# A fp32 encoder trunk on one core: warming PE without ACT, summing a weight by transfers in the last product, and another order for the last rows and for the step behind the attention

## The chip, the cores and the metric

The kernel runs on one core of one Trainium2 chip. The metric is the device time of one execution in microseconds; a lower one is better. Three runs of the kernel before took 1899.04, 1899.11 and 1897.82 us, with a median of 1899.04. The engines are called as the profile calls them: PE multiplies matrices, DVE works elementwise, ACT evaluates functions and scaled copies, POOL and SP are used here only to issue transfers (POOL those that add to what lies in the target).

## The reference

The input is one sequence of 512 tokens of 1024 float32 features. Two layers run one after the other:

```python
x += 1/2 * SwiGLU(RMSNorm(x))                       # 1024 -> 2 x 2816 -> 1024
x += W_o(g_na * NA(h) W_na + g_f * FNet(h) W_f)     # h = RMSNorm(x)
x += 1/2 * SwiGLU(RMSNorm(x))
```

NA is attention of 8 heads over a neighbourhood in a grid of 8 x 64 tokens, with a learned bias; FNet is the real part of a 2-D Fourier transform; `g_na` and `g_f` are sigmoid gates. At the end stands one more RMSNorm with a gain: out = x * rsqrt(mean(x^2) + 1e-6) * gain. Everything is float32.

## The kernel before

**Products.** A float32 product is made of three matmuls: each operand is split into a rounded part (`hi`) and the rest (`lo`), and PE adds hi x hi, hi x lo and lo x hi (L470, L471, L473 in `product`, L294 to L296 in `mm3`). The large products use Strassen's scheme: seven products in place of eight, each of sums of blocks, with results in the groups of PSUM banks that the profile calls A, B, C (in the mixer) and o (in the out products).

**Weights.** All weights come in granules of 128 x 1024 floats, in one written order (`stage_items`, the nested `strassen` writes the order of the seven products). `Stream` walks it: `load` issues the transfer from SP (`raw`, L147), `prep` makes `whi` on ACT (L178, or L173 for a negated one) and `wlo` on DVE (L181 or L174). Three buffers exist for each of `whi` and `wlo`, and weights are prepared two items ahead of the product that reads them. Some weights are sums of two granules. There are three ways to make them: a load with a second transfer that POOL issues with accumulation (L149); an addition on DVE (`summed`, L163); or, with `then`, an accumulating transfer that POOL issues behind the `wlo` of an earlier item that used the same granule (L183), so that the granule d + a of product 6 becomes d + a + b for product 3. `dma=True` chooses the last way; in `before` the mixer's products use it and the FFN's do not.

**Order of instructions.** A scheduler orders each engine's instructions; inside `tc.manual_schedule` the engines named keep the order of the code, and `tc.issue_after` puts a block behind a given instruction.

**Stages.** Each layer has an FFN, the mixer and another FFN. `stage_ffn` runs the five column groups of the inner layer, then the out products, in the passes (1), (2), (5, 6, 7, 3), (4), each over three chunks c = 0 to 2 of the inner dimension; `update` adds a result to `x` (L701). In the last FFN (`late`) the end is the final norm: `squares` sums x^2 by ACT (L337), `inverse` gives the factor of a block of 128 rows by a square root on ACT and small DVE operations (L389 to L404), `gained` multiplies x by the gain on DVE (L961), `scaled` multiplies that by the factor on ACT and sends it out (L966, L967), and `whole` does both multiplications on DVE (L973, L974). The last product runs block by block (`by_block`), so that row blocks 0 and 1 finish last, one behind the other.

**End of the attention.** In `stage_mixer`, the results of the last two attention heads are split on ACT (L1284) and DVE (L1287) into `o`; two weights of the out projection of the attention (`fill`, two granules n) are prepared; and the operands t1, t2, t3 of the gates' Strassen products are made from blocks of the normed input: a difference `t` on DVE (L1418), its `hi` on ACT (L1641), its `lo` on DVE (L1646). In the rest of the text wlo1 and wlo2 are the two weights of the fill, whi3 and whi4 those of the gates' first product, and so on in the order of the stream. Behind the fill follow the gates' products A, B, C (`gate_block`); ACT takes snapshots of the PSUM results (`sn`, L540).

**Start.** L128 to L135: `ones` and `warm` are set by DVE, ACT loads its function table with a tanh that writes into `warm`, and nine matmuls of `warm` by itself keep PE busy until the first weights and the first parts of the transposed input (`xt`) are there.

Of the kernel before, what the change touches and what calls it, by code (L numbers as in the profile page):

```python
# [17 lines left out]
P = 128  # L18
D = 1024
T = 512  # L20
L = 2
# [5 lines left out]
NH, DH = 8, 64  # L27
EPS = 1e-6
NEG = -1.0e30
WARM = 9  # L30
AHEAD = 2
ORDER = (1, 5, 2, 6, 7, 3, 4)
FETCH = 8
# [56 lines left out]
def encoder_kernel(  # L90
# [15 lines left out]
    def nm(s):  # L106
        uid[0] += 1
        return f"{s}_{uid[0]}"
# [17 lines left out]
    idents = cp.tile([P, 2, P], F32, tag="ident", name="ident")  # L126
    ident, mirror = idents[:, 0, :], idents[:, 1, :]
    ones = cp.tile([P, 1], F32, tag="ones", name="ones")  # L128
    V.memset(ones, 1.0)
    warm = slot(BF16, "warm", (T,))  # L130
    V.memset(warm, 0.0)
    S.activation(warm[:, 0:1], ones, AF.Tanh)
    pw = bank()
    for _ in range(WARM):
        PE.matmul(pw, warm[:, 0:P], warm, start=True, stop=True)  # L135
# [50 lines left out]
    def stage_items():  # L186
        items, st = [], 0

        def add(*a, **k):
            items.append(Item(*a, stage=st, **k))  # L190

        def strassen(s, name, idx, sizes, order, dma=False, behind=None):
            def key(q, g):
                return (s, name(q), idx, g) if g < 2 else (s, "h" + q, idx, 0)

            r = {}
            for q, q2 in (("a", None), ("b", None), ("c", "a"), ("d", "c")):
                r[q] = [Raw(key(q, g), n, q2 and key(q2, g)) for g, n in enumerate(sizes)]
            d2 = [Raw(key("d", g), n) for g, n in enumerate(sizes)]
            for m in order:  # L200
                for g in range(len(sizes)):
                    a, b, c, d = [r[q][g] for q in "abcd"]
                    if m == 1:
                        add(a, neg=True)
                    elif m == 2:
                        add(b)
                    elif m == 3:
                        add(d, None if dma else b)
                    elif m == 4:
                        add(d2[g])  # L210
                    elif m == 5:
                        add(d)
                    elif m == 6:
                        add(d, a, then=b.key if dma else None)
                    else:
                        add(c)
                for key in (behind or {}).get(m, ()):
                    add(Raw(key))

        def out_sizes(c):  # L220
            return (1024, 512) if c == 0 else (1024, 1024)

        def ffn(s):
            first = not items
            if first:
                for g in range(4):
                    add(Raw((s, "cl", g)), parts=2 if g < 2 else 1, pieces=2 if g == 0 else 1)
            for j in range(NB):
                order = (1, 2, 5, 6, 7, 3, 4) if first and j == 0 else (1, 5, 6, 2, 7, 3, 4)
                strassen(s, lambda q: q, j, (1024,) * (2 if first or j else 3), order)  # L230
            for order in ((1,), (2,), (5, 6, 7, 3), (4,)):
                for c in range(3):
                    strassen(s, lambda q: "o" + q, c, out_sizes(c), order)

        for l in range(L):
            ffn((l, 1))
            st += 1
            s = (l, 0)
            two = (1024, 1024)
            qk = [(s, "qk", g) for g in range(8)]  # L240
            strassen(s, lambda q: "u" + q, 0, two, (1, 5, 6, 2, 3, 7, 4), True, behind={5: qk[0:1], 6: qk[1:2], 2: qk[2:3], 3: qk[3:4], 7: qk[4:5]})
            for key in qk[5:] + [(s, "f", g) for g in range(4)]:
                add(Raw(key))
            st += 1
            for g in range(2):
                add(Raw((s, "n", 0, g)))
            st += 1
            for i in range(2):
                strassen(s, lambda q: "g" + q, i, two, ORDER, True)
            for g in range(2):  # L250
                add(Raw((s, "n", 1, g)))
            strassen(s, lambda q: "w" + q, 0, two, ORDER, True)
            ffn((l, 2))
        return items

    class Stream:
# [27 lines left out]
        def next(self, ahead=AHEAD):  # L284
            self.prep(self.pos + 1 + ahead)
            it = self.items[self.pos]
            self.pos += 1
            return it.out
# [288 lines left out]
    def stage_ffn(norm, nxt, late):  # L577
# [120 lines left out]
        def update(ps, i, j, sign, bs=(0, 1)):  # L698
            for b in bs:
                v = x[:, 2 * j + b, i * T : (i + 1) * T]  # L700
                V.scalar_tensor_tensor(v, ps[b], 0.25 * sign, v, ALU.mult, ALU.add)  # L701
# [155 lines left out]
        for i, (m, c, _) in enumerate(steps):  # L857
# [24 lines left out]
            make(i + 2)  # L882
            if i == 6 and not late:
                nxt.quad(0, 0)
            if m == 4 and c == 1:
                update(ps[1], 1, 0, 1)
            if m == 4 and c == 0 and late:
                gf[0] = slot(F32, "gf", (D,))
                nc.sync.dma_start(out=gf[0], in_=bass.AP(tensor=gfin.tensor, offset=gfin.offset, ap=[[0, P], [1, D]]))
            if c < 2:  # L890
                continue
            if m == 1:
                update(ps[1], 0, 0, -1)
            elif m == 2:
                update(ps[2], 0, 0, 1)
                nxt.squares(0, 0)
            elif m == 5:
                update(ps[5], 0, 1, 1)
                update(ps[5], 1, 1, -1)
            elif m == 6:  # L900
                update(ps[1], 1, 1, 1)
            elif m == 7:
                update(ps[7], 1, 1, 1)
                nxt.squares(1, 1)
                update(ps[1], 0, 1, -1)
            elif m == 3:
                update(ps[3], 0, 1, 1)
                nxt.squares(0, 1)
                if late:
                    make(i + 3)  # L910
            elif late:
                with (
                    tc.issue_after(ws.items[-1].last.ins),
                    tc.manual_schedule(engines={mybir.EngineType.DVE, mybir.EngineType.Activation}),
                ):
                    ready = nxt.inverses(2)
                    next(ready)
                    gained(2, 0)
                    next(ready)
                    gained(2, 1)  # L920
                    for _ in ready:
                        pass
                    scaled(nxt, 2)
                    update(ps[7], 1, 0, 1, (0,))
                    nxt.squares(1, 0, (0,))
                    root = [nxt.inverse(b, *nxt.terms(b)) for b in range(2)]
                    next(root[0])
                    gained(3, 0)
                    gained(3, 1)
                    scaled(nxt, 3)  # L930
                    update(ps[7], 1, 0, 1, (1,))
                    nxt.squares(1, 0, (1,))
                    next(root[1])
                    next(root[0])
                    gained(0, 0)
                    next(root[0])
                    gained(0, 1)
                    scaled(nxt, 0)
                    next(root[1])
                    next(root[1])  # L940
                    whole(nxt, 1, 0)
                    whole(nxt, 1, 1)
            else:
                update(ps[7], 1, 0, 1)
                if not nxt.mix:
                    nxt.squares(1, 0)
                nxt.later((1, 0))
# [4 lines left out]
    def half(tb, i=None):  # L952
        c = slice(0, D) if i is None else slice(i * T, (i + 1) * T)
        return ob[tb][:, c], x[:, tb, c], gf[0][:, c], out[:, tb, c]

    def gained(tb, i):

        if tb not in ob:
            ob[tb] = slot(F32, "o", (D,))
        o_, v, g, _ = half(tb, i)  # L960
        V.tensor_tensor(o_, v, g, ALU.mult)  # L961

    def scaled(norm, tb):

        o_, _, _, to = half(tb)
        S.activation(o_, o_, AF.Copy, scale=norm.inv[tb])  # L966
        nc.sync.dma_start(out=to, in_=o_)  # L967

    def whole(norm, tb, i):
        if tb not in ob:  # L970
            ob[tb] = slot(F32, "o", (D,))
        o_, v, g, to = half(tb, i)
        V.scalar_tensor_tensor(o_, v, norm.inv[tb], g, ALU.mult, ALU.mult)  # L973
        nc.sync.dma_start(out=to, in_=o_)  # L974


    def stage_mixer(l, norm, nxt):
# [454 lines left out]
        with tc.manual_schedule(engines={mybir.EngineType.DVE, mybir.EngineType.Activation}):  # L1432
            with tc.manual_schedule(engines={mybir.EngineType.PE}):
# [194 lines left out]
                pt_[7] = [h() for h in ph]  # L1628
                ws.prep(ws.pos + 1)
                f_copy(1, 3, rows_of(yf, 3, second_f), True)  # L1630
                t12, _ = next(first)
                o.append(hilo("o"))
                po = [att_pv(i, pt_.pop(i)) for i in (6, 7)]
                att_split(6, po[0])
                att_split(7, po[1])
        ws.prep(ws.pos + 2)
        acts = {1: (hx[0], lx[0], 0), 2: (hx[1], lx[1], 0), 3: (hx[1], lx[1], 256), 4: (hx[0], lx[0], 256)}

        def high(src, s):
# [285 lines left out]
```

## Time and profile before

| What | us |
|---|---|
| median of three runs | 1899.04 |
| profiled execution, whole time | 1898.17 |
| profiled execution, span | 1896.4 |
| PE busy | 1884.2 (99%) |
| DVE busy | 1647.8 (87%) |
| ACT busy | 1189.4 (63%) |
| POOL busy | 171.5 (9%) |
| mean granted clock of PE | 0.999 |

A line of the time order reads: start in us from the span's start, duration in us, engine, line of the kernel, operation, output <- inputs, shapes, and x with the number of instructions that are taken together. Where the engine stood idle before, a bracket gives for how long and what released it. In the rows of transfers the duration is that of issuing; how long one takes to land stands in a line of its own, as minimum, median and maximum.

### The profile page before, as it was taken

What the parts mean: (1) busy time and instruction counts of PE and PEld (TensorE: products, weight loads), DVE (VectorE), ACT (ScalarE), POOL (GpSimd) and SP (SyncE); (2) the same over time, 40 slices, a digit from 0 to 9 for tenths busy, and PEclk for the clock granted to TensorE, in tenths of its full rate; (3) what the DMA queues carried; (4) which work ended last, traced back from release to release, by engine and by line L of the source; (5) the groups of instructions that cost most, each with busy time, mean ns of one, the idle gap of its engine ahead of it and who ended that gap; (6) DMA issues with size and microseconds to landing.
All of it is one profiled execution on the core that took longest, in us unless ns stands there. A gap on an engine that the chain in (4) does not pass through costs nothing.

```text
span 1896.4 us, 25088 instructions
## 1 busy us (share of the span) xinstructions
PE 1884.2 (99%) x9149; PEld 1579.3 (83%) x9149; DVE 1647.8 (87%) x2006; ACT 1189.4 (63%) x1700; POOL 171.5 (9%) x210
## 2 busy tenths in 40 slices
PE   9999999999999999999999999999999999999998
PEld 7888888888888888888888888888888888888886
DVE  7877899788989977889997778998989899887898
ACT  6655665668666755566665556666685576556664
POOL 0101011100111011001010100101001101100010
PEclk9999999999999999999999999999999999999999
DMA  9777498932886777649877664988248767766594
GB/s 302 202 201 194 148 247 265 225 106 97 248 218 165 183 188 205 175 154 263 250 184 213 185 181 152 268 273 204 84 139 238 206 167 179 207 175 178 173 283 137
DMA packets 106939, 372.74 MB, mean 197 GB/s; under 512 B 12288, under 2 KB 12416, under 8 KB 106816
## 3 DMA queue, kind: packets, MB, share of 16 engines
q1 hardware_dynamic: 78144, 272.80, 41.9%
q0 software_dynamic: 28528, 98.33, 28.4%
q8 instruction: 71, 1.16, 0.2%
q14 instruction: 52, 0.43, 0.1%
q10 hardware_dynamic: 144, 0.02, 0.0%
HBM read 365.85 MB, written 2.11 MB: 194 GB/s over the span
## 4 chain that ended last, share of the span: by engine, by line
PE 98%; DVE 1%; issue 0%; ACT 0%; DVEq 0%; ACTq 0%
PE A L470 10%; PE A L471 10%; PE A L473 10%; PE o L470 7%; PE o L473 7%; PE o L471 7%; PE B L470 5%; PE B L471 5%; PE B L473 5%; PE ps L295 4%; PE ps L294 4%; PE ps L296 3%; PE C L471 2%; PE C L470 2%; PE C L473 2%; PE tr L593 2%
## 5 line engine op out<-in xcount | busy, mean ns | idle before, releaser
L178 ACT ACTIVATE whi<-raw 128x1024 fp32r<-128x1024 f32 (+1 forms) x536 | 553.6, 1037 | 387.1 <-PE A L471 123.4
L181 DVE TENSOR_TENSOR wlo<-raw,whi 128x1024 fp32r<-128x1024 f32 (+1 forms) x536 | 636.2, 1193 | 167.7 <-ACT whi L178 166.1
L149 POOL DMA_DIRECT2D raw<-in_wst_dram x166 | 144.4, 895 | 1375.5 <-DMA raw<-in_wst_dram 846.1
L163 DVE TENSOR_TENSOR raw<-raw,raw 128x1024 f32<-128x1024 f32 (+1 forms) x150 | 177.5, 1191 | 1.2
L471 PE MATMUL A<-whi,xl 128*128 128x512 f32 x400 | 155.7, 389 | 0.0
L470 PE MATMUL A<-whi,xh 128*128 128x512 f32 x400 | 155.7, 389 | 0.0
L473 PE MATMUL A<-wlo,xh 128*128 128x512 f32 x400 | 115.1, 389 | 0.0
L173 ACT ACTIVATE whi<-raw 128x1024 fp32r<-128x1024 f32 (+1 forms) x83 | 85.8, 1036 | 43.0 <-PE o L471 12.8
L174 DVE SCALAR_TENSOR_TENSOR wlo<-raw,whi 128x1024 fp32r<-128x1024 f32 (+1 forms) x83 | 98.0, 1195 | 13.1 <-ACT whi L173 13.1
L675 ACT ACTIVATE th<-sn,rh 128x512 f32<-128x512 f32 x80 | 56.9, 714 | 69.2 <-DVE sn L545 69.2
L540 ACT ACTIVATE sn<-A 128x512 f32<-128x512 f32 x104 | 60.7, 588 | 46.4 <-PE A L473 46.3
L473 PEld LDWEIGHTS A<-wlo,xh 128*128 128x128 f32 x400 | 75.1, 188 | 15.6
L471 PEld LDWEIGHTS A<-whi,xl 128*128 128x128 f32 x400 | 75.1, 188 | 15.4
L470 PEld LDWEIGHTS A<-whi,xh 128*128 128x128 f32 x400 | 75.1, 188 | 15.4
L470 PE MATMUL C<-whi,xh 128*128 128x512 f32 x208 | 81.1, 390 | 0.0
L471 PE MATMUL C<-whi,xl 128*128 128x512 f32 x208 | 81.0, 389 | 0.0
L471 PE MATMUL B<-whi,xl 128*128 128x512 f32 x208 | 81.0, 389 | 0.0
L470 PE MATMUL B<-whi,xh 128*128 128x512 f32 x208 | 80.9, 389 | 0.0
L473 PE MATMUL C<-wlo,xh 128*128 128x512 f32 x208 | 59.8, 389 | 0.0
L473 PE MATMUL B<-wlo,xh 128*128 128x512 f32 x208 | 59.8, 389 | 0.0
L470 PE MATMUL B<-whi,t5h 128*128 128x512 f32 x136 | 54.2, 399 | 0.0
L695 DVE TENSOR_TENSOR at<-at,at 128x1024 f32<-128x1024 f32 (+1 forms) x48 | 53.8, 1130 | 0.0
(446 smaller groups left out, 4783.9 us busy)
## 6 DMA issues: line engine op xcount, KB each, us to landing
raw<-in_wst_dram SPq DMA_DIRECT2D x470, 512.0 KB, 5.3
raw<-in_wst_dram POOLq DMA_DIRECT2D x174, 512.0 KB, 8.0
raw<-in_wst_dram SPq DMA_DIRECT2D x30, 256.0 KB, 3.9
bm<-in_bias_dram SPq DMA_DIRECT2D x16, 384.0 KB, 3.8
vs<-v SPq DMA_DIRECT2D x12, 256.0 KB, 3.8
x<-in_xin_dram SPq DMA_DIRECT2D x4, 512.0 KB, 10.2
raw<-in_wst_dram POOLq DMA_DIRECT2D x8, 256.0 KB, 8.1
dft<-in_dft_dram POOLq DMA_DIRECT2D x8, 256.0 KB, 4.2
```

The costliest lines, as they stand in the source:

```text
L149: G.dma_start(out=self.t, in_=wst[GRAN_AT[self.plus]][:, 0 : self.n], accum_op=ALU.add)
L163: V.tensor_tensor(self.raw.t, self.raw.t, self.add.t, ALU.add)
L173: S.activation(hi, t, AF.Copy, scale=-1.0)
L174: self.last = V.scalar_tensor_tensor(lo, t, -1.0, hi.bitcast(F32), ALU.mult, ALU.subtract)
L178: S.activation(hi[:, cs], t[:, cs], AF.Copy)
L181: self.last = V.tensor_tensor(lo[:, cs], t[:, cs], hi[:, cs].bitcast(F32), ALU.subtract)
L294: PE.matmul(ps, lh, rh, start=start, stop=False, skip_group_check=again)
L295: PE.matmul(ps, lh, rl, start=False, stop=False, skip_group_check=again)
L470: PE.matmul(ps, lh, rh, start=start, stop=False, skip_group_check=again)
L471: PE.matmul(ps, ll, rh, start=False, stop=False, skip_group_check=again)
L473: PE.matmul(ps, lh, rl, start=False, stop=stop, skip_group_check=again)
L540: S.activation(t[:, b, :], ps[b], AF.Copy)
```

## The change

- `WARM` goes from 9 to 10. `warm` is set ahead of `ones`, and the tanh writes into a small tile `sq` instead of `warm`, so the warm matmuls no longer read anything that ACT wrote.
- In the last FFN, the out products' chunk c = 2 uses `dma=True`: product 3's weights d + a + b come by two transfers of POOL (L183) instead of two loads by SP and two additions by DVE (L163).
- At the end of the last FFN, the gain's products for row blocks 2 and 3 (`gained`) move ahead of the last weight; the update of ps[1] moves from chunk 1 of product 4 to the end, one half for each block; row blocks 2 and 3 are scaled by ACT; of row block 0, ACT scales one half and DVE (a new `tensor_scalar`) the other; of row block 1, DVE finishes one half (`whole`) and ACT scales the other and issues its output transfer itself. Outputs go by SP as two transfers of 512 KB and three of 256 KB and by ACT as one of 256 KB; before, they were three of 512 KB and two of 256 KB, all by SP.
- In the mixer, `ws.prep(ws.pos + 2)` moves ahead of the split of the last two heads, and `next(first)`, which issues the subtraction `t`, behind it.

```diff
-WARM = 9
+WARM = 10
...
-    V.memset(ones, 1.0)
     warm = slot(BF16, "warm", (T,))
     V.memset(warm, 0.0)
-    S.activation(warm[:, 0:1], ones, AF.Tanh)
+    V.memset(ones, 1.0)
+    S.activation(sp.tile([P, 8], F32, tag="sq", name=nm("sq"), bufs=2)[:, 0:1], ones, AF.Tanh)
...
-                    strassen(s, lambda q: "o" + q, c, out_sizes(c), order)
+                    strassen(s, lambda q: "o" + q, c, out_sizes(c), order, last and c == 2)
...
-            ffn((l, 2))
+            ffn((l, 2), l == L - 1)
...
-            if m == 4 and c == 1:
+            if m == 4 and c == 1 and not late:
                 update(ps[1], 1, 0, 1)
             if m == 4 and c == 0 and late:
...
+                with (
+                    tc.issue_after(ws.items[ws.prepped - 1].last.ins),
+                    tc.manual_schedule(engines={mybir.EngineType.DVE}),
+                ):
+                    for tb in (2, 3):
+                        gained(tb, 0)
+                        gained(tb, 1)
...
                     next(ready)
-                    gained(2, 0)
                     next(ready)
-                    gained(2, 1)
+                    gained(0, 0)
                     for _ in ready:
                         pass
                     scaled(nxt, 2)
+                    scaled(nxt, 3)
+                    update(ps[1], 1, 0, 1, (0,))
+                    root = [nxt.inverse(b, *nxt.terms(b)) for b in range(2)]
                     update(ps[7], 1, 0, 1, (0,))
                     nxt.squares(1, 0, (0,))
-                    root = [nxt.inverse(b, *nxt.terms(b)) for b in range(2)]
                     next(root[0])
-                    gained(3, 0)
-                    gained(3, 1)
-                    scaled(nxt, 3)
+                    gained(0, 1)
+                    gained(1, 0)
+                    update(ps[1], 1, 0, 1, (1,))
                     update(ps[7], 1, 0, 1, (1,))
                     nxt.squares(1, 0, (1,))
                     next(root[1])
                     next(root[0])
-                    gained(0, 0)
                     next(root[0])
-                    gained(0, 1)
-                    scaled(nxt, 0)
+                    scaled(nxt, 0, 0)
+                    o_, _, _, to = half(0, 1)
+                    V.tensor_scalar(o_, o_, nxt.inv[0], None, ALU.mult)
+                    nc.sync.dma_start(out=to, in_=o_)
                     next(root[1])
                     next(root[1])
-                    whole(nxt, 1, 0)
                     whole(nxt, 1, 1)
+                    scaled(nxt, 1, 0, nc.scalar)
...
-    def scaled(norm, tb):
-
-        o_, _, _, to = half(tb)
+    def scaled(norm, tb, i=None, by=nc.sync):
+
+        o_, _, _, to = half(tb, i)
         S.activation(o_, o_, AF.Copy, scale=norm.inv[tb])
-        nc.sync.dma_start(out=to, in_=o_)
+        by.dma_start(out=to, in_=o_)
...
                 f_copy(1, 3, rows_of(yf, 3, second_f), True)
-                t12, _ = next(first)
                 o.append(hilo("o"))
                 po = [att_pv(i, pt_.pop(i)) for i in (6, 7)]
+                ws.prep(ws.pos + 2)
                 att_split(6, po[0])
                 att_split(7, po[1])
-        ws.prep(ws.pos + 2)
+                t12, _ = next(first)
```

More of the change, by code (lines that the diff above doesn't have):

```diff
@@ L221, in out_sizes, with ffn @@
             return (1024, 512) if c == 0 else (1024, 1024)
-        def ffn(s):
+        def ffn(s, last=False):
             first = not items
```

## The prediction

> **What bounds the kernel now.** I read the shares of the page first, then the waits of PE, then the time order of each engine at the four places that the change touches. The profiled execution took 1898.17 us (span 1896.4 us), 0.87 us below the median of the three runs shown, 1899.04 us; the sum below is made against the execution and set on the median.
>
> ```profile
> PE 1884.2 (99%) x9149; PEld 1579.3 (83%) x9149; DVE 1647.8 (87%) x2006; ACT 1189.4 (63%) x1700; POOL 171.5 (9%) x210
> PE ps L135 <- ACT warm L132: 2.7, 1, 2.7
> ```
>
> PE is busy 99%; its only listed wait is the one at the start, and 8.9 us separate its end (1887.5, where DVE's last wait on it ends, quoted below) from the span's. So a saving on DVE, ACT, SP or POOL is worth nothing unless it shortens the start or what follows PE's last product, while a delay of a weight or a snapshot past the matmul that needs it is added in full: nothing later gives it back. I take the four places in order of time.
>
> **Start: 0 us.** The zeroing of `warm` goes ahead of the one of `ones`, the tanh writes another tile, and a tenth warm matmul is added.
>
> ```profile
> 0.90 0.27 DVE L131 MEMSET warm<- 128x256 uint32 x1
> 2.73 4.02 PE L135 MATMUL ps<-warm 128*128 128x512 bf16 x9 [2.73 <-ACT warm L132]
> 4.81 0.61 ACT L178 ACTIVATE whi<-raw 128x512 fp32r<-128x512 f32 x1
> 6.19 0.99 PE L470 MATMUL cl<-whi,xh 128*128 128x512 f32 x1
> 8.57 0.73 ACT L303 ACTIVATE xh<-xt,gn 128x512 fp32r<-128x512 f32 x1 [2.31 <-DMA xt<-in_xtr_dram]
> 9.33 0.75 DVE L304 SCALAR_TENSOR_TENSOR xl<-xt,gn,xh 128x512 fp32r<-128x512 f32 x1
> 10.14 0.19 PEld L471 LDWEIGHTS cl<-whi,xl 128*128 128x128 f32 x1 [0.35 <-DVE xl L304]
> ```
>
> PE's warming then starts at about 0.81+0.27 = 1.1 instead of 2.73. Ten matmuls at 4.02/9 = 0.45 us end near 5.6, after the first weights are ready (4.81+0.61 = 5.42), so real work starts some 0.6 us before 6.19. It then runs into the wait that already stands at 10.14: the second part of `xt` lands (8.57), ACT makes `xh`, DVE makes `xl` (9.33+0.75 = 10.08). Neither the transfer nor the two operations move, so the 0.6 us becomes idle time ahead of 10.14. The tenth matmul (0.45 us) lies in the same gap. Bounds: all of the 0.6 if the wait went too, +0.3 if the tenth matmul held back what the wait leaves; the row of the wait decides for 0.
>
> **Behind the attention, once in each layer: +1.9 us each, +3.8 us together.** No word of the change's summary names it, but the subtraction `t` (L1418) and the preparation of the fill's second weight change places. On DVE the order wlo1, t, o x4, wlo2, wlo3 becomes wlo1, wlo2, o x4, t, wlo3. ACT's order up to whi6 stays: whi2, o x4, t1h, whi3, (DVE's block) t2h, whi4, fs x4, whi5, whi6. Layer 1:
>
> ```profile
> 478.90 1.72 DVE L1287 TENSOR_TENSOR o<-ps,o 64x256 fp32r<-64x256 f32 x4
> 481.79 1.22 DVE L174 SCALAR_TENSOR_TENSOR wlo<-raw,whi 128x1024 fp32r<-128x1024 f32 x1
> 492.91 2.36 DVE L181 TENSOR_TENSOR wlo<-raw,whi 128x1024 fp32r<-128x1024 f32 x2 [1.62 <-ACT whi L178]
> 502.00 2.52 DVE L181 TENSOR_TENSOR wlo<-raw,whi 128x1024 fp32r<-128x1024 f32 x2
> ```
>
> ```profile
> 476.84 1.07 ACT L178 ACTIVATE whi<-raw 128x1024 fp32r<-128x1024 f32 x1
> 479.37 1.06 ACT L1641 ACTIVATE t1h<-t 128x1024 fp32r<-128x1024 f32 x1
> 487.84 1.06 ACT L1641 ACTIVATE t2h<-t 128x1024 fp32r<-128x1024 f32 x1 [6.46 <-DVE t L1656]
> 488.80 1.05 ACT L173 ACTIVATE whi<-raw 128x1024 fp32r<-128x1024 f32 x1
> 491.80 2.03 ACT L178 ACTIVATE whi<-raw 128x1024 fp32r<-128x1024 f32 x2
> 510.60 1.06 ACT L178 ACTIVATE whi<-raw 128x1024 fp32r<-128x1024 f32 x1 [0.31 <-PE A L471]
> 511.56 0.58 ACT L540 ACTIVATE sn<-A 128x512 f32<-128x512 f32 x1
> ```
>
> Step by step: whi2 ends at 477.91, so wlo2 runs from 477.95 and `o` follows at 479.1 for 1.72; `t` starts at 480.84 and ends at 482.06 (before: its result was there when ACT reached t1h at 479.37). t1h goes to 482.1 (+2.7), whi3 behind it to 483.1, and wlo3, which needs whi3, to 484.16 against 481.79: +2.37. The three windows below (us, then busy us of PE, weight loads, DVE, ACT, POOL) show DVE without a hole in what follows:
>
> ```profile
> 476.60:491.20 14.60, 14.49 (x68) 11.68 (x67) 14.46 (x16) 8.05 (x13) 1.71 (x2) 1.00 1.05 307
> 493.00:504.50 11.50, 11.50 (x52) 9.52 (x51) 11.43 (x10) 8.04 (x10) 0.85 (x1) 1.00 0.49 147
> 1857.00:1882.60 25.60, 25.60 (x115) 21.20 (x114) 25.60 (x30) 13.23 (x19) 0.00 (x0) 1.00 0.29 98
> ```
>
> So t2h (487.84) and whi4 behind it (488.80) also come 2.37 later, whi4 ending at 492.2; whi5 goes from 491.80 to 494.1, ends at 495.2, and wlo5 starts there, 2.3 after 492.91. From there DVE had no hole up to wlo9 (502.00): +2.25. Behind its wlo9 hangs POOL's transfer:
>
> ```profile
> 503.51 0.85 POOL L183 DMA_DIRECT2D raw<-in_wst_dram  x1 [16.38 <-DVE wlo L181]
> 1444.00 0.85 POOL L183 DMA_DIRECT2D raw<-in_wst_dram  x1 [19.59 <-DVE wlo L181]
> DMA to landing us min/median/max: 6.8/7.7/8.6
> DMA to landing us min/median/max: 5.5/7.7/12.6
> ```
>
> ```profile
> 491.81 0.39 PE L470 MATMUL A<-whi,xh 128*128 128x512 f32 x1
> 494.53 0.39 PE L470 MATMUL B<-whi,t1h 128*128 128x512 f32 x1
> 512.21 0.49 PE L470 MATMUL A<-whi,t3h 128*128 128x512 f32 x1
> ```
>
> The first landing line is for the two L183 transfers of this place, the second for all sixteen. What PE sees: in the fill it can gain up to the 0.1 us that it lacks in the first window, since wlo2 comes early; at 491.81 it waits for whi4 until 492.2, +0.4; at 494.53 it waits for whi5 until 495.2, +0.7 in all. At 512.21 PE had no slack: it waits for the second snapshot (511.56), which on ACT stands behind the weight (510.60) that waits for POOL's transfer. Issued at 505.75 and landing 6.8 us later, at 512.5, it gives whi until 513.5, the snapshot until 514.1, PE at 514.1: +1.9. That contains the 0.7. Layer 2 runs the same code 940.5 us later (its POOL transfer at 1444.00), so +3.8 us for both.
>
> Bounds: the landing has the widest spread. With 5.5 us PE goes on at 512.9, and what stands is the +0.7 of B: +0.7 per layer. With the median of all, 7.7, it is +2.9, with 8.6 it is +3.8. I take 6.8, the row of this very transfer. Below nothing lies only the fill's 0.1. The Trainium skill, "DMA: Bandwidth & Descriptors", section "Anatomy of one DMA — SWDGE (gpsimd) path", gives such a transfer 2.0 us and its bytes over 436 GB/s, an estimate of 3.2 us for 512 KB; by it the transfer would be off the path and the two layers would cost 1.4 us, but the rows have 5.5 at the least.
>
> **Last out product, c = 2: 0 us.** The two additions L163 leave DVE, SP loses two loads of 512 KB, POOL gains two accumulating transfers behind product 6's weights.
>
> ```profile
> 1853.50 1.22 DVE L181 TENSOR_TENSOR wlo<-raw,whi 128x1024 fp32r<-128x1024 f32 x1
> 1860.17 1.22 DVE L163 TENSOR_TENSOR raw<-raw,raw 128x1024 f32<-128x1024 f32 x1
> 1878.04 3.49 DVE L181 TENSOR_TENSOR wlo<-raw,whi 128x1024 fp32r<-128x1024 f32 x3
> ```
>
> ```profile
> 1884.16 0.62 PE L473 MATMUL o<-wlo,c4h 128*128 128x512 f32 x2
> ```
>
> DVE has no hole in the third window above and saves 2 x 1.14 us; four products with the gains of rows 2 and 3 (4 x 0.6 us), which stood behind the last weight, now stand ahead of it. So that weight ends near 1882, as before, about 2 us ahead of the last pair of matmuls at 1884.16 that reads it. The first transfer starts behind product 6's wlo (1853.50 + 1.22), about 1855, the second some 2 us later; with 5.5 to 8.6 us the first lands between 1860.5 and 1863.6, where the sum that it replaces ended at 1861.4. PE has no wait there now; what is late first is the last weight, with 2 us of cover. SP's and POOL's queues have nothing else due in that stretch that PE waits for.
>
> **Behind the last product: -1.0 us.** Here every DVE operation counts.
>
> ```profile
> 1887.54 0.69 DVE L701 SCALAR_TENSOR_TENSOR x<-o,x 128x512 f32<-128x512 f32 x1 [0.33 <-PE o L473]
> 1888.33 0.67 DVE L961 TENSOR_TENSOR o<-x,gf 128x512 f32<-128x512 f32 x1
> ...
> 1890.83 1.42 DVE L973 SCALAR_TENSOR_TENSOR o<-x,inv,gf 128x512 f32<-128x512 f32 x2
> 1891.67 1.21 SPq L974 DMA_DIRECT2D out_dram<-o  x2
> ```
>
> Two products with the gain (0.6 each, the one at 1888.33 and a second like it) leave the stretch behind 1887.54, one of the two L973 halves (0.6) goes to ACT, and one 128x512 product by `inv` (0.6) comes in: -1.2. The moved update of ps[1] (0.6) stands just ahead of the last one and may delay it by 0.1. DVE's last half then ends near 1891.1 and its output is issued there, against 1892.27 (the second of the two issues at 1891.67): -1.1. ACT's two halves of 0.6 us should end by 1891, and the one that ACT issues itself lands with the other. I take -1.0. Bounds: -1.2 if ACT stays clear, +0.5 if ACT's two halves and its own issue end last.
>
> **Sum.** 0 + 3.8 + 0 - 1.0 = +2.8 us: the profiled execution would take 1901.0 and, set on the median, 1901.8 us (+0.15%). About 0.2% (3.8 us: 1895.2 to 1902.8) is what a measurement of this kernel can tell from no change, so the likeliest answer is "same", near its upper end.
>
> **The rivals.** Slower: the accumulating transfer lands late. Its place is POOL's issue near 505.75 and its twin near 1446; each us of landing is a us per layer. It decides from a landing of 7.2 us (2.3 per layer): barely above the 6.8 forecast, and below the 7.7 median. At 7.7 the sum is 2 x 2.9 - 1.0 = +4.8, 1903.8 us; at 8.6, 1905.6. For it: the median, and that SP's loads, held back by the same weights, then run beside it; against it: both transfers of the nearest place took under 7. Chance 0.33.
>
> Cheap: the transfer lands early, or the second snapshot doesn't stand behind it, and only B's +0.7 is left: 1.4 - 1.0 = +0.4, 1899.4 us. For it the 5.5 row; chance 0.13.
>
> Faster: the wait for t1h is no wait, the layers gain the fill's 0.1 each, and the tail gives its -1.2: -1.4, 1897.6 us, still within 0.2%. The start would have to give its whole 1.6 us of earlier warming, and more, to pass the bound. Against it stand the 10.14 wait and DVE's closed row. Chance 0.08, a third of it past the bound.
>
> Late last weight: product 3's transfers take over 9 us, ACT's weights come 1 to 2 us late and the last weight uses up its cover; +1 us on the forecast, 1902.8. Chance 0.04.
>
> **How the numbers follow.** The forecast has 0.42. Within 0.2%: 0.42 + 0.13 + 0.05 + 0.02 = 0.62; slower: 0.33 + 0.02 = 0.35; faster: 0.03. The range runs from the faster rival, 1897.6, to the 8.6 us landing, 1905.6. The likeliest one's own range is 1900.8 to 1902.8.
>
> **What will show it.** In the changed profile: warm matmuls from 1.1 and the `xl` wait still near 10.1; t1h at 482.1 with an idle time of over 2 us before it, released by DVE `t`; wlo3 at 484.2; a PE wait of over 1 us near 512, released by ACT's snapshot, in both layers; PE's end near 1891.3; no L163 at 1860 to 1864; the last SP issue 3.6 us after PE's end instead of 4.8. Wrong it would be if ACT made t1h without that wait, if the transfer landed clearly off 6.8 us, or if PE waited between 1860 and 1887.

## The result and the profile after

The changed kernel took 1903.72 us (median of 10 runs, 1902.30 to 1905.44) against 1899.23 us (10 runs) for the kernel before: a ratio of 1.0023 with a 95% interval of 1.0015 to 1.0032, so +4.5 us. The forecast was 1901.8 with a range of 1897.6 to 1905.6: the time lies in the range and on the side that was forecast, but past the 1902.8 (0.2%) at which the likeliest case ended. The profiled execution took 1902.30 us, 4.13 us more than the one of before.

Behind the attention, layer 1. The first fence has the waits of PE in the changed kernel (in all us, times, longest), the others the time order of DVE, ACT, POOL and PE there.

```profile
PE A L470 <- ACT sn L540: 1.4, 2, 0.8
PE A L470 <- ACT whi L173: 1.4, 2, 0.7
PE o L473 <- DVE wlo L181: 0.3, 1, 0.3
```

```profile
479.87 1.23 DVE L1427 TENSOR_TENSOR t<-t,t 128x1024 f32<-128x1024 f32 x1
483.17 1.23 DVE L174 SCALAR_TENSOR_TENSOR wlo<-raw,whi 128x1024 fp32r<-128x1024 f32 x1 [2.08 <-ACT whi L173]
```

```profile
481.13 1.06 ACT L1650 ACTIVATE t1h<-t 128x1024 fp32r<-128x1024 f32 x1 [2.76 <-DVE t L1427]
490.19 1.04 ACT L173 ACTIVATE whi<-raw 128x1024 fp32r<-128x1024 f32 x1
511.34 1.06 ACT L178 ACTIVATE whi<-raw 128x1024 fp32r<-128x1024 f32 x1 [1.13 <-DMA raw<-in_wst_dram]
512.30 0.58 ACT L540 ACTIVATE sn<-A 128x512 f32<-128x512 f32 x1
```

```profile
504.90 0.85 POOL L183 DMA_DIRECT2D raw<-in_wst_dram  x1 [18.72 <-DVE wlo L181]
```

```profile
491.28 0.50 PE L470 MATMUL A<-whi,xh 128*128 128x512 f32 x1 [0.67 <-ACT whi L173]
494.31 0.50 PE L470 MATMUL B<-whi,t1h 128*128 128x512 f32 x1
512.93 0.50 PE L470 MATMUL A<-whi,t3h 128*128 128x512 f32 x1 [0.65 <-ACT sn L540]
```

This execution is 0.99 us ahead at the fill, because of its start (below). With that added, t1h starts at 482.12 (forecast 482.1), wlo3 at 484.16 (484.16), POOL's transfer is issued at 505.89 (505.75), and PE goes on at 513.92 (514.1). The chain came out as it was laid out: ACT waits 2.76 us for DVE's `t`, DVE 2.08 us for whi3, ACT 1.13 us for the landing, PE for the snapshot. The landing took 6.33 us where 6.8 was forecast, and PE followed it by 1.70 where 1.6 was.

The last out product and the end. First the window up to PE's end in the kernel before and the one in the changed kernel (us, then busy us of PE, weight loads, DVE, ACT and POOL), then rows of the changed kernel from the time order of the four engines and SP's queue, the rows between left out.

```profile
1857.00:1887.50 30.50, 30.50 (x135) 24.93 (x133) 29.95 (x45) 15.76 (x25) 0.00 (x0) 1.00 0.27 92
1861.00:1891.20 30.20, 29.89 (x130) 23.88 (x129) 28.50 (x45) 15.34 (x22) 0.86 (x1) 1.00 0.32 88
```

```profile
1868.15 1.23 DVE L181 TENSOR_TENSOR wlo<-raw,whi 128x1024 fp32r<-128x1024 f32 x1 [1.12 <-ACT whi L178]
1869.82 2.01 ACT L178 ACTIVATE whi<-raw 128x1024 fp32r<-128x1024 f32 x2 [1.70 <-DMA raw<-in_wst_dram]
1884.13 2.48 DVE L970 TENSOR_TENSOR o<-x,gf 128x512 f32<-128x512 f32 x4
1886.54 1.21 DVE L181 TENSOR_TENSOR wlo<-raw,whi 128x1024 fp32r<-128x1024 f32 x1
1887.80 0.73 PE L473 MATMUL o<-wlo,c4h 128*128 128x512 f32 x2 [0.31 <-DVE wlo L181]
1890.65 0.61 PE L473 MATMUL o<-wlo,c4h 128*128 128x512 f32 x2
1892.22 1.48 DVE L701 SCALAR_TENSOR_TENSOR x<-o,x 128x512 f32<-128x512 f32 x2
1896.54 0.33 SPq L983 DMA_DIRECT2D out_dram<-o  x1
```

DVE, which was idle for 0.55 us of this stretch before (30.50 - 29.95), now stands idle for 1.70 us of it (30.20 - 28.50), above all for weights that ACT makes from POOL's two transfers; the four products with the gain come next, the last weight is made at 1886.54, PE waits for it, and when PE ends (1891.28) DVE's last two updates have not begun: the first starts at 1892.22. The last output issue stands 5.26 us behind PE's end; before it was 4.76.

The next table sets the starts of the same matmuls in two traces against each other: by how many us PE falls behind (or, with a minus, gets ahead of) the first look at the kernel before, place by place. A look is one profiled execution; "exchange alone" and "exchange undone" are the first and the fifth experiment.

| Place | after | after, 2nd look | exchange alone | exchange undone | before, 2nd look |
|---|---|---|---|---|---|
| start (up to 30 us) | -0.94 | -0.54 | -0.69 | -1.00 | -0.56 |
| 30 us to the fill, layer 1 | -0.05 | +0.07 | +0.23 | +0.39 | +0.09 |
| fill, layers 1 and 2 | -0.37, -0.38 | -0.39, -0.36 | -0.34, -0.38 | 0, 0 | 0, 0 |
| whi4 and whi5, layers 1 and 2 | +1.27, +1.33 | +1.30, +1.27 | +1.25, +1.30 | 0, 0 | 0, 0 |
| second t3h block, layers 1 and 2 | +0.82, +0.97 | +1.27, +0.72 | +1.37, +1.48 | 0, +0.91 | 0, +0.68 |
| between the layers' places | +0.33 | -0.15 | -0.12 | -0.05 | +0.09 |
| 1453 to 1875 us | -0.04 | +0.05 | -0.05 | +0.09 | +0.13 |
| last product, c = 2 | +0.83 | +0.78 | +1.25 | +0.06 | +0.14 |
| behind PE | +0.36 | +0.33 | -0.05 | +0.33 | -0.01 |
| end of the span | +4.13 | +4.35 | +5.25 | +0.73 | +0.54 |

### The profile page after: what moved, and what is told of

Same layout as the page of the kernel before. It is cut to its first block, busy times and chain, and to the rows that moved or that the text cites. A ratio compares the mean times of both kernels' runs of the same rounds, so it can differ in the third digit from the quotient of the medians.

```text
span 1900.5 us, 25094 instructions
## 1 busy us (share of the span) xinstructions
PE 1886.2 (99%) x9150; PEld 1578.8 (83%) x9150; DVE 1645.6 (87%) x2005; ACT 1188.6 (63%) x1701; POOL 173.4 (9%) x212
## 4 chain that ended last, share of the span: by engine, by line
PE 93%; issue 2%; DMA 2%; DVE 1%; ACT 0%; POOL 0%; SPq 0%; POOLq 0%; DVEq 0%; ACTq 0%
PE A L470 10%; PE A L471 10%; PE A L473 9%; PE o L470 7%; PE o L471 7%; PE o L473 7%; PE B L470 5%; PE B L471 5%; PE B L473 5%; PE ps L294 3%; PE ps L295 3%; PE ps L296 3%; PE C L471 2%; PE C L470 2%; PE C L473 2%
## 5 line engine op out<-in xcount | busy, mean ns | idle before, releaser
L163 DVE TENSOR_TENSOR raw<-raw,raw 128x1024 f32<-128x1024 f32 (+1 forms) x148 | 174.8, 1189 | 1.2
```

The lines of the kernel that those rows point to most:

```text
L163: V.tensor_tensor(self.raw.t, self.raw.t, self.add.t, ALU.add)
```

## The experiments

The ratios are the recorded ones, with their 95% intervals; they are not the quotients of the two medians beside them and differ from these by up to 0.0005.

**The exchange alone.**

```diff
                 f_copy(1, 3, rows_of(yf, 3, second_f), True)
-                t12, _ = next(first)
                 o.append(hilo("o"))
                 po = [att_pv(i, pt_.pop(i)) for i in (6, 7)]
+                ws.prep(ws.pos + 2)
                 att_split(6, po[0])
                 att_split(7, po[1])
-        ws.prep(ws.pos + 2)
+                t12, _ = next(first)
```

> The kernel before with the exchange behind the attention alone. Theory M (the prediction's step: t1h waits for t, and the second snapshot of product A waits behind the weight that POOL's transfer brings): +3.4 to +3.8 us, PE 1.7 to 1.9 us later at the second t3h block of each layer, nothing elsewhere. Rival (the delay comes from other places that the changed kernel shifted too, and the exchange itself is covered): under +1.5 us.

Measured: 1903.43 us against 1898.63, ratio 1.0028 (1.0017 to 1.0039): as much as the whole change. The table has 2.28 and 2.40 us for the two layers, more than the 1.7 to 1.9 expected. It also has +1.25 us in the last product, which no theory had; there PE waited for another operand:

```profile
PE o L471 <- DVE c4l L301: 0.9, 1, 0.9
```

**The start alone.**

```diff
-WARM = 9
+WARM = 10
...
-    V.memset(ones, 1.0)
     warm = slot(BF16, "warm", (T,))
     V.memset(warm, 0.0)
-    S.activation(warm[:, 0:1], ones, AF.Tanh)
+    V.memset(ones, 1.0)
+    S.activation(sp.tile([P, 8], F32, tag="sq", name=nm("sq"), bufs=2)[:, 0:1], ones, AF.Tanh)
```

> The kernel before with the warming's edit alone. Theory as predicted (the wait for xl behind the second xt transfer still sets the time): 0 +- 0.3 us, PE's later work where it was. Rival, from the changed kernel's trace, where that transfer landed 1.7 us earlier and PE was 0.9 us ahead from 22 us on: -0.6 to -1.0 us.

Measured: 1898.58 against 1898.63, ratio 1.0003 (0.9994 to 1.0011). PE in the time order:

```profile
5.56 0.50 PE L470 MATMUL cl<-whi,xh 128*128 128x512 f32 x1 [0.47 <-ACT whi L178]
9.59 0.50 PE L470 MATMUL cl<-whi,xh 128*128 128x512 f32 x1 [0.98 <-ACT xh L303]
10.38 0.51 PE L471 MATMUL cl<-whi,xl 128*128 128x512 f32 x1 [0.28 <-DVE xl L304]
```

Real work starts 0.63 us earlier and waits 0.98 and 0.28 us for the second `xt` part, as forecast. What moves the start is that transfer: ACT used it at 8.57, 8.82 and 8.59 us in three looks and between 6.65 and 7.78 in the eleven others. Against the first look at the kernel before, PE was 0.03 to 0.84 us ahead at 30 us in the eight early looks without the edit and 0.54 to 1.00 in the three with it. So most of the -0.94 of the first look at the changed kernel is the transfer; a few tenths may be the edit where the transfer is early.

**The transfers alone**, the end as before. `last` comes in as in the change: a parameter of `ffn`, true for the last FFN.

```diff
-                    strassen(s, lambda q: "o" + q, c, out_sizes(c), order)
+                    strassen(s, lambda q: "o" + q, c, out_sizes(c), order, last and c == 2)
```

> The kernel before with product 3's weights for c = 2 summed by POOL's transfers, the end as before. Predicted: 0 us. Rival, from the changed kernel's trace (ACT waited there for the landings, then the last weights came late): PE waits 0.2 to 0.7 us for the last weights and DVE is later at the end, +0.3 to +1.5 us.

Measured: 1898.66 against 1898.63, ratio 1.0000 (0.9991 to 1.0008), and no wait of PE is listed in the last product (it loses 0.25 us there). As forecast.

**The new end alone**, DVE summing as before: all hunks of the change in `stage_ffn` and `scaled`, of which the first two are

```diff
-            if m == 4 and c == 1:
+            if m == 4 and c == 1 and not late:
                 update(ps[1], 1, 0, 1)
...
+                    for tb in (2, 3):
+                        gained(tb, 0)
+                        gained(tb, 1)
```

> The kernel before with the new end alone, product 3's weights summed by DVE as before. Predicted for the end: -1.0 us. Rival, from the changed kernel's trace (four products with the gain stand ahead of the last weight and two updates behind it, so DVE is still behind when PE ends): the last update 1 to 2 us behind PE's end or PE waiting for the last weight, +0.3 to +2 us.

Measured: 1899.67 against 1898.63, ratio 1.0006 (0.9997 to 1.0015): by time undecided, but not the -1.0 forecast. The profile has the place. DVE's order behind the last weight:

```profile
1879.92 2.50 DVE L970 TENSOR_TENSOR o<-x,gf 128x512 f32<-128x512 f32 x4
1882.32 1.22 DVE L181 TENSOR_TENSOR wlo<-raw,whi 128x1024 fp32r<-128x1024 f32 x1
...
1886.80 1.29 DVE L970 TENSOR_TENSOR o<-x,gf 128x512 f32<-128x512 f32 x2
1888.02 1.48 DVE L701 SCALAR_TENSOR_TENSOR x<-o,x 128x512 f32<-128x512 f32 x2
```

PE ended at 1887.13 (0.38 ahead of before); the two last updates start at 1888.02 and the span ends 0.17 us later behind PE than before.

**The change without the exchange**: the changed kernel, with the hunk of the first experiment taken back.

```diff
-                ws.prep(ws.pos + 2)
                 att_split(6, po[0])
                 att_split(7, po[1])
-                t12, _ = next(first)
+        ws.prep(ws.pos + 2)
```

> The changed kernel with the exchange behind the attention undone. Theory M (the exchange makes all of the difference, the start gives nothing, the transfers give DVE room for the new end): -1.0 to +0.3 us against the kernel before, PE's shift under 0.3 us from 470 to 1870 us beyond what the start's landings give. Rival (the last product's late weights, seen as 0.5 and 1.1 us of waits of PE in the two profiles that have the exchange, come from the transfers and the new end): +0.7 us or more, PE waiting again near 1880.

(`t12, _ = next(first)` stands behind `f_copy` again.) Measured: 1899.01 against 1898.92, ratio 0.9996 (0.9987 to 1.0005). Theory M holds: with the exchange gone, so is the difference. Its profile has PE losing 0.9 us at the second t3h block of layer 2, where the kernel has no exchange: the transfer took 7.9 us there. The second look at the kernel before has the same (below). At the end, the window up to PE's end and the last weight are

```profile
1857.00:1887.90 30.90, 30.90 (x137) 25.13 (x135) 28.89 (x45) 15.68 (x23) 0.86 (x1) 1.00 0.33 93
```

```profile
1883.15 1.22 DVE L181 TENSOR_TENSOR wlo<-raw,whi 128x1024 fp32r<-128x1024 f32 x1
```

DVE is idle for 2.01 us here too, and yet PE loses only 0.05 us in the last product.

**Half of the exchange**: the second weight early, `t` where it was.

```diff
                 t12, _ = next(first)
                 o.append(hilo("o"))
                 po = [att_pv(i, pt_.pop(i)) for i in (6, 7)]
+                ws.prep(ws.pos + 2)
                 att_split(6, po[0])
                 att_split(7, po[1])
-        ws.prep(ws.pos + 2)
```

> The kernel before with half of the exchange: the fill's second weight is prepared ahead of the split of the last heads, but t stays ahead of both (DVE: wlo1, t, wlo2, o x4, wlo3; ACT as before). Theory M (the price is that t1h waits for t): t1h stays near 479.4, no wait of PE for whi4 nor for the second snapshot, the fill's gain of 0.37 us in each layer stays: -0.3 to -0.8 us. Rival (the price is the split of the last heads behind wlo2): +1 us or more, with PE waiting in the fill for o.

Measured: 1899.56 against 1898.92, ratio 0.9999 (0.9990 to 1.0008); PE gains 0.17 and 0.15 us in the two fills, not 0.37, and waits nowhere behind them. So neither the early weight nor the later split costs anything that shows; the price comes with moving `t`.

**`t` between the weight and the split.**

```diff
-                t12, _ = next(first)
                 o.append(hilo("o"))
                 po = [att_pv(i, pt_.pop(i)) for i in (6, 7)]
+                ws.prep(ws.pos + 2)
+                t12, _ = next(first)
                 att_split(6, po[0])
                 att_split(7, po[1])
-        ws.prep(ws.pos + 2)
```

> The exchange with t between wlo2 and o x4 (DVE: wlo1, wlo2, t, o x4, wlo3), so that t ends about 1.3 us later than before instead of 3.1. Theory M, by the wait: t1h comes about 0.9 us later instead of 2.7, less than the 1.6 us that DVE has idle before wlo5, but whi4 and whi5 still 0.6 to 0.9 us late against 0 to 0.5 us of room: +0.3 to +1.5 us in both layers together. Rival (any move of wlo2 ahead of o costs the same): +3 us or more.

Measured: 1899.44 against 1898.92, ratio 1.0001 (0.9992 to 1.0011). In the profile t1h waits 0.99 us and whi4 and whi5 are in time; at the second t3h block PE loses 0.99 and 0.70 us, net of the fills 0.61 and 0.30:

```profile
479.81 1.06 ACT L1641 ACTIVATE t1h<-t 128x1024 fp32r<-128x1024 f32 x1 [0.99 <-DVE t L1418]
510.67 1.06 ACT L178 ACTIVATE whi<-raw 128x1024 fp32r<-128x1024 f32 x1 [1.30 <-DMA raw<-in_wst_dram]
```

So a third of the wait (0.99 of 2.76 us) costs a fifth to a quarter of the time (0.9 of 3.7 and 4.7 us): the price follows the wait for `t`. POOL's transfer was issued at 503.57, which is 0.98 us later than before (503.51) when PE's lead of 0.92 us is added. This profile too has a wait for c4l in the last product (1.1 us), though its exchange is small.

**The landing taken out of the chain.** The exchange, and in the first gate block product 3's weight summed by DVE; and the same without the exchange as a control.

```diff
-                strassen(s, lambda q: "g" + q, i, two, ORDER, True)
+                strassen(s, lambda q: "g" + q, i, two, ORDER, i > 0)
```

> The exchange alone, and in the first gate block product 3's weight summed by DVE (L163) from a second load instead of POOL's transfer behind wlo9, so that nothing between t1h and the second snapshot waits for a landing; DVE gets 2 x 1.14 us more in each layer. Theory M: PE's wait at the second t3h block (+0.8 to +1.5 us in each layer) goes, the +0.9 us at B stays: +1.2 to +2.4 us against the kernel before, 2.4 to 3.6 less than the exchange alone. Rival (ACT's and DVE's order alone makes the second wait): +4 us or more as with the exchange alone.

> The kernel before with product 3's weight of the first gate block summed by DVE from a second load, as in the run that joined this with the exchange; it is that run's control. Theory M: +1.5 to +3 us against the kernel before from the sums and loads alone, in the gates behind the first block, so that the exchange costs 1.9 us there (0.96 in each layer) instead of 3.6 to 4.7. Rival: 0 +- 0.5 us, so that the exchange would cost its 4 us without any landing in its chain.

Measured: with the exchange 1903.45 against 1898.92, ratio 1.0021 (1.0012 to 1.0031); the control 1900.07 against 1899.05, ratio 1.0005 (0.9996 to 1.0014). At the second t3h block of the first gate block the loss is gone (+0.05 and +0.06 us, where the exchange alone has +1.37 and +1.48), as theory M says. Its total is wrong all the same: PE loses 4.0 us at the same place of the second gate block of layer 1, which still uses POOL's transfer (2.35 by the wait below, the rest by a slower clock behind it), and 1.1 us there in layer 2. The control is between its two expectations by the interval (-0.8 to +2.7 us); its profile's span is only 0.1 us longer than before, as the rival has it.

```profile
555.24 0.50 PE L470 MATMUL A<-whi,t3h 128*128 128x512 f32 x1 [2.19 <-ACT sn L540]
```

The next table has that place in layer 1 for the four kernels, on the clock of the kernel before (PE's shift at 540 us taken off). PE comes there at 552.24; the fourth column adds to the landing the 1.70 us that PE follows it by (below).

| Look | first L183 issued | to landing | landing + 1.70 | PE loses, clock aside |
|---|---|---|---|---|
| before | 541.50 | 6.81 | 550.01 | 0 |
| exchange alone | 543.01 | 7.34 | 552.05 | 0 |
| DVE's sums alone (control) | 543.34 | 7.59 | 552.63 | 0.4 |
| both | 544.62 | 8.27 | 554.59 | 2.35 |

The slack of 2.2 us just covers the exchange, and almost covers the sums, which delay DVE by about as much; it does not cover both with a landing that was 1.5 us slower. So the run shows that the loss sits where a landing ends DVE's delay, and that it goes when that landing goes; what the exchange would cost with no landing behind it at all is not shown, because the sums bring a delay of their own.

**The new end with less for DVE**: the four early products with the gain are left out, and ACT scales `x` itself, so rows 256 to 511 of the output lack the gain.

```diff
                     for tb in (2, 3):
-                        gained(tb, 0)
-                        gained(tb, 1)
+                        ob[tb] = slot(F32, "o", (D,))
...
-        S.activation(o_, o_, AF.Copy, scale=norm.inv[tb])
+        S.activation(o_, x[:, tb, :] if tb > 1 else o_, AF.Copy, scale=norm.inv[tb])
```

> The new end alone, with the four products of x and the gain for row blocks 2 and 3 left out (ACT scales x itself, so the output of these rows lacks the gain): DVE has 2.4 us less to do ahead of the last weight, the rest of the end is as in the change. Theory T (the new end gains nothing because DVE, without a hole, is 1.3 to 1.7 us behind when PE ends): the last update starts under 0.2 us behind PE's end as before, and from PE's end to the end of the span it is 1.0 to 1.2 us less than before (7.7 to 7.9 against 8.9): -0.8 to -1.2 us. Rival (ACT's two halves, its own output issue or the landings set the end): under 0.4 us gained, with the last update on time.

Measured: 1898.06 against 1899.05, ratio 0.9995 (0.9986 to 1.0003); by time undecided, by the profile clear. PE ends at 1887.17; the chain and the last issue:

```profile
1887.19 0.69 DVE x L701
```

```profile
1890.72 0.33 SPq L982 DMA_DIRECT2D out_dram<-o  x1
```

The last update starts with PE's end, and the last issue stands 3.55 us behind it (before 4.76, the new end with all its work 5.2). From PE's end to the span's end it is 1.39 us less than before. Theory T holds: the new order behind the last product is shorter, and DVE's queue ahead of it eats that.

**Both kernels once more.**

> The kernel before once more, for the spread of the landings. The second xt part's use on ACT is either near 7.0 or near 8.7 us, whatever the kernel; the first L183 transfer of each layer lands 6.0 to 7.9 us after its issue; no wait of PE near 1880 us if the last product's late weights come with the change, and one of about 1 us in some looks if they come by chance.

> The changed kernel once more, for the spread. By theory M, PE goes on at the second t3h block 1.70 us behind the first L183 landing in both layers, with a wait of 0.7 to 1.7 us, and waits for whi4 and whi5 before it (1.1 to 1.3 us in all, after the 0.4 us gained in the fill). The start near 0 or near -0.9 us by the xt landing; PE's wait near 1880 us is again there if it belongs to the change.

Measured: 1899.58 and 1902.51 us, one execution each, and the first table's columns. The landings (6.2 to 7.7 us), the 1.70 us and the waits for whi4 and whi5 came as expected. The second `xt` part was used at 7.63 and 7.22 us, so it is not either near 7.0 or near 8.7. The loss in the last product came again with the change (+0.78) and not without it (+0.14). The kernel before waited at the second t3h block of layer 2 this time:

```profile
1452.96 0.50 PE L470 MATMUL A<-whi,t3h 128*128 128x512 f32 x1 [0.50 <-ACT sn L540]
```

Where PE waited, it went on a fixed time behind the landing of the first L183 transfer:

| Look | L183 issued | to landing | landed | PE goes on | behind landing |
|---|---|---|---|---|---|
| after, layer 1 | 504.90 | 6.33 | 511.23 | 512.93 | 1.70 |
| after, layer 2 | 1447.43 | 6.52 | 1453.96 | 1455.66 | 1.70 |
| after 2nd, layers 1 and 2 | 505.42, 1447.93 | 6.79, 6.24 | 512.21, 1454.17 | 513.91, 1455.87 | 1.70, 1.70 |
| exchange alone, layers 1 and 2 | 505.42, 1448.08 | 6.91, 7.00 | 512.32, 1455.08 | 514.02, 1456.78 | 1.70, 1.70 |
| `t` in the middle, layers 1 and 2 | 503.57, 1445.05 | 7.00, 6.70 | 510.57, 1451.75 | 512.27, 1453.44 | 1.70, 1.69 |
| exchange undone, layer 2 | 1443.34 | 7.89 | 1451.23 | 1452.93 | 1.70 |
| end with less for DVE, layer 1 | 502.99 | 7.40 | 510.38 | 512.09 | 1.71 |
| before 2nd, layer 2 | 1443.60 | 7.66 | 1451.26 | 1452.96 | 1.70 |

## Why the prediction was right or wrong

**Start, 0 us: right within what can be told.** The edit alone gave no difference (1.0003, 0.9994 to 1.0011), and with a late transfer what the earlier warming wins is lost at the wait for `xl`. What I took for fixed is not: ACT could use the second `xt` part up to 1.9 us earlier in most looks, with the edit or without it, and in the looks at the changed kernel PE's list has no wait for `xl` at all.

**Behind the attention, +1.9 us in each layer: right.** The two looks at the changed kernel have 1.72 and 1.92, and 2.18 and 1.63 us (the sums of the table's fill, whi4 and whi5, and second t3h rows), 1.86 in the mean; alone the exchange cost +4.8 us and taken back it left no difference. Inside it two terms moved against each other: the fill gave 0.37 instead of the 0.1 that I allowed, and whi4 and whi5 cost 1.27 to 1.33 (0.9 net of the fill) instead of 0.7. The landing was forecast at 6.8 and took 6.2 to 6.8, and PE followed it by 1.70 where I had 1.6. That POOL's transfer is the cause was only half right: it is the place where DVE's lateness is paid. With the transfer gone from the first gate block the loss there is gone too (+0.05 and +0.06), but DVE, later still by the sums, then makes the second block's transfer late.

**Last out product, 0 us: wrong, +0.8 us.** The step that failed is "that weight ends near 1882, as before, about 2 us ahead of the last pair of matmuls". It rests on DVE saving 2 x 1.14 us, and the transfers gave no such room: in the stretch up to PE's end DVE idled 2.01 us with the change without the exchange and 1.70 us in the changed kernel, 0.55 before. With PE's shift taken off, the last weight ended at 1881.5 before, at 1883.0 with the transfers alone, at 1883.9 with the new end alone and at 1884.0 with both and no exchange. The four early products moved it by their 2.4 us, and the transfers took nothing of that back. So the cover of 2 us was used up, without any cost yet (+0.06 us in the last product). In the changed kernel (PE's shift 2.95 us) the weight was made from 1883.6 to 1884.8, and the pair at 1884.16 waited. The rival of the late last weight, to which I gave 0.04 and +1 us, had the place and the size, but not the cause: the two transfers took 7.5 and 8.3 us, not over 9, and 7.6 and 8.6 us in the look without the exchange, where PE did not wait.

What came on top is late loads: SP's load that stood at 1844.79 in the first look at the kernel before was issued 1.5 and 2.1 us later than PE's shift in the two looks at the changed kernel, 1.9 and 2.0 us later with the exchange alone and with `t` in the middle, and 0 to 0.8 us later in the nine other looks. In these four PE lost 0.8 to 1.4 us in the last product, in no other more than 0.3. All four have `t` behind the early weight, as has a fifth that lost nothing much (the exchange with DVE's sums, +0.2). In the two of them with the end as before, ACT and DVE run this section in the same order as in the kernel before, and in all four the loads up to 1833 us are issued on time to 0.01 us; only the landings before that differ, in every look. How an exchange 350 us earlier would bring it, or whether four of five is chance, stays open.

**Behind the last product, -1.0 us: wrong, +0.35 us.** The step that failed is "two products with the gain (0.6 each) leave the stretch behind 1887.54", counted at its full 1.2 us. They left it for a place ahead of PE's end where DVE had 0.33 us to spare, and it was late there. Behind PE's end DVE starts five large operations in the kernel before (an update, two products with the gain, two L973 halves) and again five with the new end alone (a product with the gain, two updates, a product by `inv`, one half); the two last updates start 0.9 and 1.7 us behind PE's end there and in the changed kernel. With the four early products left out it starts three, and the end is 1.39 us shorter than before. So the order is shorter only where DVE arrives in time; as it is, the end is a little longer.

**The sum.** +3.8 for the exchange came out as +3.7 in the mean of the two looks; 0.8 and 1.35 us were missing in the two last steps. That makes 4.9 us without the start, for 4.5 by the medians. The rival that went over 0.2% by a late landing had the right side for the wrong reason: no landing of the exchange took over 7.0 us in the looks with it. That the profiled PE ended at 1891.28, where 1891.3 was forecast, is luck: 0.9 us gained at the start and 0.8 us lost in the last product cancel.

## To carry to other kernels

When two instructions change places on one engine, follow every later instruction of the other engine's fixed order behind the first one that now waits; here one subtraction, 3 us later, delayed ACT's next conversion, DVE's next weight, a transfer behind that weight and a snapshot behind that transfer, and the matrix engine paid at two places. Work moved from behind the end to ahead of it is saved only as far as its engine has idle time there; count the idle us of that stretch first. And when work on a late engine replaces a transfer, it makes the next transfer behind that engine later too: add up the delays and set them against the slack of the next chain.

## What the runs showed of the hardware

The transfer that POOL issues with accumulation (512 KB) took between 6.0 and 7.9 us to land at one and the same place of the program, in twelve looks at ten kernels. In the kernel before this spread alone decides whether PE waits there not at all or loses 0.7 us. The Trainium skill, "DMA: Bandwidth & Descriptors", section "Anatomy of one DMA — SWDGE (gpsimd) path", would have 3.2 us by the estimate in the prediction; no look came near it.

A wait of 2.19 us was followed by a lower granted clock of PE, in the run with the exchange and DVE's sums. The windows before, in and behind it (PE's clock is the third number from the end):

```profile
552.60:555.20 2.60, 0.45 (x2) 0.03 (x1) 0.47 (x1) 1.56 (x3) 0.00 (x0) 1.00 1.02 307
555.20:559.40 4.20, 4.16 (x11) 3.31 (x12) 1.66 (x2) 1.99 (x2) 0.57 (x1) 0.59 0.55 197
559.50:566.00 6.50, 6.50 (x30) 5.37 (x29) 5.95 (x8) 3.07 (x3) 1.05 (x2) 1.00 0.89 182
```

The clock was 0.59 in the mean of the 4.2 us behind the wait; PE lost 2.35 us by the wait and its restart and 1.5 us more by the slower clock. The Trainium skill, "TensorE: Matmul & The Clock Gate", section "What's actually happening", has the clock fall after an idle window of about 3.4 us; this wait is shorter. The waits of up to 1.3 us at the second t3h block in the other looks left the clock at 1.00.
